# A hybrid decoder layer in fp32r: the moving operand of every wide matmul read by turns from two pieces

## The chip, the cores and the metric

The kernel runs on one core of one Trainium2 chip. The metric is the device time of one execution in microseconds (us). In the profile, PE is the matrix engine (TensorE), PEld its weight loads, DVE is VectorE, ACT is ScalarE, POOL is GpSimd and SP is SyncE, which issues most of the DMAs. L835 means line 835 of the kernel.

## The reference, cut to what matters

One layer (DEPTH is 1) on 1024 tokens of width 1024, all in float32:

```python
h = rms_norm(x, mix_norm)
z = h @ w_in                     # 1024 x 2320: gq gk gv gr glr sq sk sv
o_gla = rms_norm(gla_chunked(gq, gk, gv, log_a), gla_norm) * silu(gr)     # 4 heads
o_swa = swa_sink_attention(rms_norm(sq, q_norm), rms_norm(sk, k_norm), sv, sinks)   # window 128
x = x + concat([o_gla, o_swa]) @ w_out
u = causal_dwconv(rms_norm(x, ffn_norm) @ w_up, conv_w, conv_b)           # 1024 x 5632
a, bval = split(u, 2)
return x + (silu(a) * bval) @ w_down                                      # 2816 x 1024
```

## The kernel before, in words

The tokens are eight row tiles of 128. A matmul has a stationary operand of 128 x 128, which a weight load brings in ahead of it, and a moving operand of up to 512 columns, which is streamed past it; the result goes to a PSUM bank of 512 fp32 values. For accuracy each fp32 operand of a large matmul is split into a high part, rounded to the type fp32r, and the rest (`split`, line 92, and `tr_hi`/`tr_lo`, lines 250 and 258), and a product takes three passes: high by high, high by low, low by high.

The work runs in this order. *Input projections* (up to about 300 us): a tile of `x` is normalised and transposed into `big` (row tile, block of 128 features, high or low, 128 tokens); `dense` (line 314) multiplies eight feature blocks of `big`, stationary, with a weight block of 512 columns (272 for `k`), moving, 24 matmuls into one bank. `unit_q`, `unit_k`, `unit_v`, `unit_g` and `unit_r` take the bank and scale, square or multiply it (`head_rms`, `q_post`, `gla_qk`, `gate`). Between them stand the steps of the attention (`swa_scores`: queries stationary, 256 keys of `kt` moving, lines 443 and 444) and of the gated linear attention. *Output projection* (about 300 to 400 us): `unit_o` adds its bank to the residual `acc` and starts the second norm. Its rows are transposed into `big` again; for tiles 4 to 7, `norm2_sums` forms sums and differences of the quadrants in PSUM and puts them into `big` and `ex`.

*Feed-forward* (about 400 us to the end): both large products are done by a Strassen-Winograd scheme of seven products for a two by two block product. Up (`product`, line 822): the weights `w` are stationary, the moving operand (`b_operand`, line 801) is four row tiles of `big` or `ex`, 4 x 128 columns out of four places 8 KB apart in a partition; twelve matmuls into one bank. `post` combines the banks, and runs the convolution and the gate on DVE and ACT. Down (`down_pair`, line 1006): the gated tokens `g` are stationary, half a row block of `w_down` (512 columns) is moving; six matmuls into two banks, which one add of DVE over 1024 elements puts into `acc` (line 1020). `last_row` does the last two blocks of `w_down` row tile by row tile, and stores.

The order of the work is written out by hand: `at` gives each step a time, and the steps are issued in the order of these times; the first ones are a fixed list. On each engine the instructions run in the order of issue, with semaphores between engines. POOL and ACT split weights ahead of their use, DVE and ACT empty the banks.

Of the kernel before, what the change touches and what calls it, by code (L numbers as in the profile page):

```python
# [34 lines left out]
def hymba_layer_kernel(ctx, tc, x, mix_norm, w_in, w_alpha2, b_alpha, gla_norm,  # L35
# [175 lines left out]
    def norm2_tr(t):  # L211
        h = fin["h", t]
        if t < 4:
            norm_tr(t, h, "n2")
            return
        pbs = fin["pb", t] = []
        for q in range(2):
            pt = bank(f"n2pt_{t}_{q}")
            for k in range(4):
                c = (q * 4 + k) * P  # L220
                pe.transpose(pt[:, k * P:(k + 1) * P], h[:, c:c + P], ident)
            pbs.append(pt.rearrange("p (k c) -> p k c", k=4))

    def norm2_sums(t):

        i, ex, pn = t - 4, fin["ex"], fin["pn"]
        p0, p1 = fin["pb", t]

        def put(src, dst):
            split(src, dst[:, :, 0, :], dst[:, :, 1, :], dve)  # L230

        b12 = pn.tile([P, 4, P], F32, tag="b12", name=f"b12_{t}", bufs=1)
        b11, b21 = big[:, i, 0:4].bitcast(F32), big[:, i, 4:8].bitcast(F32)
        act.copy(b12, p0)
        put(p1, big[:, t, 4:8])
        dve.tensor_sub(p0, p0, b11[:, :, 0, :])
        dve.tensor_sub(p0, p0, b11[:, :, 1, :])
        put(p0, big[:, t, 0:4])
        dve.tensor_sub(p1, p1, b12)
        put(p1, ex[:, 1, i])  # L240
        dve.tensor_add(p1, p1, b11[:, :, 0, :])
        dve.tensor_add(p1, p1, b11[:, :, 1, :])
        put(p1, ex[:, 0, i])
        dve.tensor_sub(p0, b21[:, :, 0, :], p1)
        dve.tensor_add(p0, p0, b21[:, :, 1, :])
        put(p0, ex[:, 2, i])

    trs = {}

    def tr_hi(t, q, h, tag):  # L250
# [5 lines left out]
        act.copy(big[:, t, q * 4:q * 4 + 4, 0, :], trs[tag, t, q])  # L256

    def tr_lo(t, q, tag):
        hi, lo = big[:, t, q * 4:q * 4 + 4, 0, :], big[:, t, q * 4:q * 4 + 4, 1, :]
        dve.tensor_sub(lo, trs[tag, t, q], hi.bitcast(F32))  # L260

    def norm_tr(t, h, tag):
        for q in range(2):
            tr_hi(t, q, h, tag)
            tr_lo(t, q, tag)


    blocks = {}
# [41 lines left out]
    def load_piece(name, c0, n, k2, engs=(None, None), hi_eng=None):  # L310
# [3 lines left out]
    def dense(t, ws, n, name):  # L314
        pb = bank(name)
        for k in range(KD):
            for i, (ra, rb) in enumerate(PASSES):
                pe.matmul(pb[:, :n], lhsT=big[:, t, k, ra, :], rhs=ws[k][:, rb, :n],  # L318
                          start=(k == 0 and i == 0), stop=(k == KD - 1 and i == 2))
        return pb  # L320


    qo = gl_q.tile([P, NT, 512], F32, name="qo")
# [31 lines left out]

    def head_rms(ps_ap, nh, t, name):
        sq = k2_tile(name + "sq")
        act.activation(sq[:, :nh * HD], ps_ap, AF.Square, scale=row_scale(t))
        ss = gl.tile([P, 8], F32, tag="hss", name=name + "ss", bufs=3)
        dve.tensor_reduce(ss[:, :nh], sq[:, :nh * HD].rearrange("p (h d) -> p h d", d=HD),  # L360
                          op=ALU.add, axis=AX.X)
        return rms_scale(ss[:, :nh], HD, nh, name, gl, f"hr{nh}")

    def q_post(t, pb):
        r = head_rms(pb, 8, t, f"q{t}")
        rs = gl.tile([P, 8], F32, tag="rs", name=f"rs{t}", bufs=2)
        dve.scalar_tensor_tensor(rs, r, row_scale(t), qscale, op0=ALU.mult, op1=ALU.mult)
        dve.tensor_tensor(
            qo[:, t, :].rearrange("p (j g d) -> p g j d", j=4, g=2),
            pb.rearrange("p (g j d) -> p g j d", g=2, j=4),  # L370
            rs.rearrange("p (g j o) -> p g j o", g=2, o=1).broadcast_to((P, 2, 4, HD)),
            ALU.mult)

# [61 lines left out]
    def swa_scores(t, g):  # L435
# [3 lines left out]
        for j in range(4):  # L439
            if j % 2 == 0:  # L440
                pbs.append(bank(f"sc{t}_{g}_{j}").rearrange("p (j s) -> p j s", j=2))
            qc, kc = slice(j * P, (j + 1) * P), slice(t * P, t * P + 256)
            pe.matmul(pbs[-1][:, j % 2, :], lhsT=q[:, g, qc], rhs=kt[:, g, kc], start=True, stop=False)  # L443
            pe.matmul(pbs[-1][:, j % 2, :], lhsT=ql[:, g, qc], rhs=kt[:, g, kc], start=False, stop=True)
        if g == 0:
            smx[t] = [gl.tile([P, 8], F32, tag=f"sm{i}", name=f"sm{i}_{t}", bufs=2) for i in range(4)]
        mx, nm, den, es = smx[t]
        pr = k4_tile(f"pr{t}_{g}").rearrange("p (j s) -> p j s", j=4)
        for j in range(4):
            h = g * 4 + j  # L450
            dve.tensor_tensor_reduce(pr[:, j, s0:], pbs[j // 2][:, j % 2, s0:], dist[:, s0:], 1.0,
                                     sinks_s[:, h:h + 1], ALU.add, ALU.max, mx[:, h:h + 1])
        hs = slice(g * 4, g * 4 + 4)
        dve.tensor_mul(nm[:, hs], mx[:, hs], slope_n[:, hs])
# [95 lines left out]
    def gla_qk(t, pb):  # L550
        ex = gex[t]
        kd = gkd[t] = gl.tile([P, 256], F32, tag="kd", name=f"kd{t}", bufs=2)
        qe = gqk[t] = k2_tile(f"qe{t}")[:, 0:256]
        for i, dst, c, e in ((1, qe, 0, 0), (0, kd, 256, 1)):
            dve.scalar_tensor_tensor(dst, pb[:, c:c + 256], row_scale(t, i), ex[:, e], op0=ALU.mult, op1=ALU.mult)

    def gla_tr(t):
        pb = bank(f"gt{t}")
# [142 lines left out]
    def unit_q_part(t, k0, k1):  # L701
        if k0 == 0:
            psb["q", t] = bank(f"dq{t}")
        pb = psb["q", t]
        for k in range(k0, k1):

            for i, (ra, rb) in enumerate(((0, 0), (1, 0), (0, 1))):
                pe.matmul(pb, lhsT=big[:, t, k, ra, :], rhs=blocks["q"][k][:, rb, :],  # L708
                          start=(k == 0 and i == 0), stop=(k == KD - 1 and i == 2))

    def q_done(t):
        q_post(t, psb.pop(("q", t)))

    def unit_q(t):
        q_post(t, dense(t, blocks["q"], 512, f"dq{t}"))
# [2 lines left out]
        kvl_post(t, dense(t, blocks["k"], 272, f"dk{t}"))  # L718

    def unit_v(t):  # L720
        act.activation(vg[0][:, t, :], dense(t, blocks["v"], 512, f"dv{t}"), AF.Copy, scale=row_scale(t))

    def unit_g(t):
        gla_qk(t, dense(t, blocks["g"], 512, f"dg{t}"))
# [4 lines left out]
    def unit_o(t, half):  # L729
# [5 lines left out]
        dve.tensor_add(acc[:, cs], acc[:, cs], pb)  # L735
        if half == 1:
            norm2_stat(t)

# [83 lines left out]
    def product(ch, name):  # L822
# [9 lines left out]
        if ch == 0:  # L832
            steps.sort(key=lambda step: step[2])
        for i, (k, ra, rb) in enumerate(steps):
            pe.matmul(pb, lhsT=w[:, ra, k, :], rhs=b_operand(bn, k, rb),  # L835
                      start=(onto is None and i == 0), stop=(i == 11), skip_group_check=onto is not None)

    def half_tile(name):
# [167 lines left out]
    def down_pair(p, k, j):  # L1006
# [6 lines left out]
        for i in range(2):  # L1013
            for n, (ra, rb) in enumerate(PASSES):
                c = (2 * j + i) * P
                pe.matmul(pb[:, i], lhsT=g[:, ra, c:c + P], rhs=w[:, rb, :],  # L1016
                          start=(onto is None and n == 0), stop=(n == 2), skip_group_check=onto is not None)
        t = 4 * th + 2 * j
        acc = fin["all"][:, t:t + 2, nh * 512:(nh + 1) * 512]
        dve.tensor_add(acc, acc, pb)  # L1020

    def w_split(ch, hf, slot):
        w = blocks["d", ch, hf] = slot_tile(slot, f"dnw{ch}_{hf}")
# [9 lines left out]
    def last_row(t):  # L1033
# [6 lines left out]
        for hf, pb in enumerate(pbs):  # L1040
            for c0, c1 in ((0, 256), (256, 512)) if (t, hf) == (NT - 1, 1) else ((0, 512),):
                for ch in (NCH - 2, NCH - 1):
                    g, w = gtiles[ch, t // 4], blocks["d", ch, hf]
                    for i, (ra, rb) in enumerate(PASSES[::-1]):
                        pe.matmul(pb[:, c0:c1], lhsT=g[:, ra, (t % 4) * P:(t % 4 + 1) * P], rhs=w[:, rb, c0:c1],  # L1045
                                  start=(ch == NCH - 2 and i == 0), stop=(ch == NCH - 1 and i == 2))
                cs = slice(hf * 512 + c0, hf * 512 + c1)
                dve.tensor_add(acc[:, cs], acc[:, cs], pb[:, c0:c1])
                sp.dma_start(out[t * P:(t + 1) * P, cs], acc[:, cs])


# [253 lines left out]
```

## Time and profile before

| | |
|---|---|
| median of 3 runs | 1033.62 us (1032.31 to 1033.64) |
| the profiled execution | 1033.08 us, its span 1031.4 us |
| granted TensorE clock, mean | 0.999 of full |
| busy share of the span | PE 99%, PEld 82%, DVE 77%, POOL 60%, ACT 47% |
| matmuls | 4976, each with a weight load of its own |
| DMA | 67.13 MB, 65 GB/s on the mean |

Matmuls are pipelined: one starts long before the one ahead has ended. So the mean duration of a matmul in the profile (389 ns for 512 columns) is a latency, and its cost is the time from its start to the start of the next. A busy time of a group is the union of its members' times.

### The profile page before, as it was taken

The numbers are of one execution on the slowest core, as the hardware profiler recorded it, in microseconds if no ns is written. First come the engines' busy times: TensorE is split into PE (matmuls) and PEld (weight loads), VectorE is DVE, ScalarE is ACT, GpSimd is POOL, SyncE is SP. The second block draws the span as 40 slices with busy tenths as digits, with TensorE's granted clock in tenths as the row PEclk, the third lists the DMA queues.
The fourth block names the chain that finished last, engine by engine and source line by source line (L and its number), as shares of the span: only waits on it lengthen the run. The fifth ranks groups of instructions, "written<-read, shape, count | busy, mean of one in ns | idle before, by whom it ended". The sixth has DMA issues, their size and how long they took to land.

```text
span 1031.4 us, 13921 instructions
## 1 busy us (share of the span) xinstructions
PE 1023.9 (99%) x4976; PEld 849.5 (82%) x4976; DVE 795.6 (77%) x1332; ACT 480.7 (47%) x988; POOL 618.3 (60%) x510
## 2 busy tenths in 40 slices
PE   9999999999999999999999999999999999999998
PEld 6899887888888888888888888888888888888887
DVE  6776667764131689797989899897979898998976
ACT  5627655445240345554444545444444444454541
POOL 4592132325560205867878797887878787978750
PEclk9999999999999999999999999999999999999999
DMA  6252113002035202112120212212121111122104
GB/s 218 61 155 62 42 45 102 21 1 83 1 101 185 62 1 82 41 42 83 41 71 33 62 41 62 62 48 75 41 82 41 63 41 44 59 62 62 42 20 163
DMA packets 67502, 67.13 MB, mean 65 GB/s; under 512 B 4648, under 2 KB 52201, under 8 KB 67434
## 3 DMA queue, kind: packets, MB, share of 16 engines
q1 hardware_dynamic: 63448, 61.27, 19.3%
q10 hardware_dynamic: 3986, 4.99, 2.0%
q8 instruction: 39, 0.64, 0.2%
q14 instruction: 29, 0.24, 0.1%
HBM read 57.33 MB, written 4.19 MB: 60 GB/s over the span
## 4 chain that ended last, share of the span: by engine, by line
PE 96%; DVE 2%; ACT 1%; DMA 0%; issue 0%; POOL 0%; ACTq 0%; SPq 0%
PE fb L835 38%; PE dn_P L1016 18%; PE do L318 8%; PE dg L318 4%; PE dr L318 4%; PE dv L318 4%; PE dq L318 3%; PE dk L318 2%; PE gb L835 2%; PE dq L708 1%; PE pv L491 1%; PE dl L1045 1%; PE fb L1045 1%; PE go L601 1%; PE ga L592 1%; PE sc L443 1%
## 5 line engine op out<-in xcount | busy, mean ns | idle before, releaser
L1016 PE MATMUL dn_P<-dw,dg 128*128 128x512 f32 x840 | 212.9, 389 | 0.0
L1020 DVE TENSOR_TENSOR acc<-acc,dn_P 128x1024 f32<-128x1024 f32 x140 | 169.7, 1213 | 55.7 <-PE dn_P L1016 55.5
L1016 PEld LDWEIGHTS dn_P<-dw,dg 128*128 128x128 f32 x840 | 157.6, 188 | 33.1 <-DVE acc L1020 0.4
L318 PE MATMUL do<-wow,big 128*128 128x512 f32 x384 | 90.9, 393 | 0.0
L97 POOL TENSOR_TENSOR dw<-dn,dw 128x512 fp32r<-128x512 f32 x50 | 68.8, 1377 | 25.1 <-ACT dw L94 24.1
L318 PEld LDWEIGHTS do<-wow,big 128*128 128x128 f32 x384 | 71.1, 188 | 14.4
L887 ACT COPY ca<-fb 128x512 f32<-128x512 f32 x62 | 36.3, 586 | 65.0 <-PE fb L835 65.0
L842 DVE SCALAR_TENSOR_TENSOR ua<-fb,cc,ua 128x511 f32<-128x511 f32 x84 | 62.2, 741 | 0.3
L835 PE MATMUL fb<-big,A11w 128*128 128x512 f32 x252 | 61.2, 389 | 0.0
L835 PE MATMUL fb<-big,A12w 128*128 128x512 f32 x252 | 60.9, 390 | 0.2 <-DVE ua L842 0.2
L835 PE MATMUL fb<-big,S4w 128*128 128x512 f32 x252 | 61.0, 389 | 0.0
L835 PE MATMUL fb<-big,S1w 128*128 128x512 f32 x252 | 61.0, 389 | 0.0
L835 PE MATMUL fb<-ex,S3w 128*128 128x512 f32 x252 | 60.9, 389 | 0.0
L835 PE MATMUL fb<-ex,S2w 128*128 128x512 f32 x252 | 60.9, 389 | 0.0
L835 PE MATMUL fb<-ex,A22w 128*128 128x512 f32 x252 | 60.5, 389 | 0.0
L835 PEld LDWEIGHTS fb<-big,A12w 128*128 128x128 f32 x252 | 47.1, 188 | 10.3 <-DVE ua L842 0.6
L835 PEld LDWEIGHTS fb<-ex,S3w 128*128 128x128 f32 x252 | 47.3, 188 | 9.8
L835 PEld LDWEIGHTS fb<-big,S1w 128*128 128x128 f32 x252 | 47.3, 188 | 9.8
L835 PEld LDWEIGHTS fb<-ex,A22w 128*128 128x128 f32 x252 | 47.3, 188 | 9.8
L835 PEld LDWEIGHTS fb<-ex,S2w 128*128 128x128 f32 x252 | 47.3, 188 | 9.8
L835 PEld LDWEIGHTS fb<-big,A11w 128*128 128x128 f32 x252 | 47.3, 188 | 9.8
L835 PEld LDWEIGHTS fb<-big,S4w 128*128 128x128 f32 x252 | 47.3, 188 | 9.8
(432 smaller groups left out, 2395.6 us busy)
## 6 DMA issues: line engine op xcount, KB each, us to landing
up<-in_w_up_dram SPq DMA_DIRECT2D x44, 512.0 KB, 3.9
dn<-in_w_down_dram SPq DMA_DIRECT2D x22, 512.0 KB, 3.5
acc<-in_x_dram SPq DMA_DIRECT2D x8, 512.0 KB, 6.6
out_dram<-acc SPq DMA_DIRECT2D x15, 256.0 KB, 2.0
xt<-in_x_dram SPq DMA_DIRECT2D x7, 512.0 KB, 3.6
vraw<-in_w_in_dram SPq DMA_DIRECT2D x4, 512.0 KB, 3.9
graw<-in_w_in_dram SPq DMA_DIRECT2D x4, 512.0 KB, 3.7
qt<-qt ACTq DMA_DIRECT2D x16, 128.0 KB, 2.2
```

What stands on the lines that cost most here:

```text
L97: (eng or pool).tensor_sub(lo, src, hi.bitcast(F32))
L318: pe.matmul(pb[:, :n], lhsT=big[:, t, k, ra, :], rhs=ws[k][:, rb, :n], start=(k == 0 and i == 0), stop=(k == KD - 1 and i == 2))
L443: pe.matmul(pbs[-1][:, j % 2, :], lhsT=q[:, g, qc], rhs=kt[:, g, kc], start=True, stop=False)
L491: pe.matmul(pbs[i][HALF[g]], lhsT=vv[rows, t - 1 + b, HALF[g]], rhs=rhs[rows, :, HALF[i]], start=start, stop=stop)
L592: pe.matmul(pb[:, pr * 256:(pr + 1) * 256], lhsT=gqt[t][:, pr, :], rhs=qbd[t % 2][:, pr], start=(pr == 0), stop=(pr == 1))
L601: pe.matmul(pb[:, h * P:(h + 1) * P], lhsT=asb[:, h, :], rhs=v[:, h * P:(h + 1) * P], start=(h == 0), stop=(t == 0 and h == 3))
L835: pe.matmul(pb, lhsT=w[:, ra, k, :], rhs=b_operand(bn, k, rb), start=(onto is None and i == 0), stop=(i == 11), skip_group_check=onto is n ...
L842: dve.scalar_tensor_tensor(dst, src, w, dst, op0=ALU.mult, op1=ALU.add)
L887: act.copy(dst, pb)
L1016: pe.matmul(pb[:, i], lhsT=g[:, ra, c:c + P], rhs=w[:, rb, :], start=(onto is None and n == 0), stop=(n == 2), skip_group_check=onto is no ...
L1020: dve.tensor_add(acc, acc, pb)
L1045: pe.matmul(pb[:, c0:c1], lhsT=g[:, ra, (t % 4) * P:(t % 4 + 1) * P], rhs=w[:, rb, c0:c1], start=(ch == NCH - 2 and i == 0), stop=(ch == N ...
```

## The change

The order in which each wide moving operand is read is altered, and the data is laid out so that the results come out right.

- Weights (`dense`, `unit_q_part`, `down_pair`, `last_row`): the 512 columns stay where they are, and are read 0, 256, 1, 257, and so on. Column c of the first half is then at place 2c of the bank, column c of the second half at 2c + 1. All that takes such a bank reads it with a step of two, first half and second half in turn, and writes in the old order.
- The `k` weights (272 columns) are put apart when they are split: even columns into the first half, odd ones into the second. Read by turns they come out in the old order, and the bank is as it was.
- The keys `kt` (256 columns, two blocks of 128) are read by turns, and the scores taken with a step of two.
- The activations of the up products: in each row tile of `big` and `ex`, even tokens stand in the first 64 places and odd ones in the last 64, for the second norm only (`parted`). The transposed tile is taken out of PSUM with a step of two, and `norm2_sums` works through such views throughout. `product` reads the two sets of a row tile by turns, so that the tokens of a bank are in the old order.

Stationary operands are read as before, and the number of instructions, waits and DMAs is as it was. The diff, cut to its core:

```diff
+    def two_streams(a):
+        return a.rearrange("p (h c) -> p c h", h=2)
+
+    def halves_of(pb):
+        return pb.rearrange("p (c h) -> p h c", h=2)
...
 norm2_sums
-            split(src, dst[:, :, 0, :], dst[:, :, 1, :], dve)
+            dst = dst.rearrange("p k r (h c) -> p k r h c", h=2)
+            split(src, dst[:, :, 0], dst[:, :, 1], dve)
...
 tr_hi
+        if parted:
+            trs[tag, t, q] = pt.rearrange("p (k c h) -> p k h c", k=4, h=2)
+        act.copy(tr_dst(t, q, 0, parted), trs[tag, t, q])
...
 piece
+            if name == "k":
+                src = halves_of(src)
+                hi, lo = (part.rearrange("p (h c) -> p h c", h=2) for part in (hi, lo))
...
 dense
-                pe.matmul(pb[:, :n], lhsT=big[:, t, k, ra, :], rhs=ws[k][:, rb, :n],
+                pe.matmul(pb[:, :n], lhsT=big[:, t, k, ra, :], rhs=two_streams(ws[k][:, rb, :n]),
...
-        return pb
+        return halves_of(pb) if n == 512 else pb
...
 swa_scores
-            pe.matmul(pbs[-1][:, j % 2, :], lhsT=q[:, g, qc], rhs=kt[:, g, kc], start=True, stop=False)
+            pe.matmul(pbs[-1][:, j % 2, :], lhsT=q[:, g, qc], rhs=two_streams(kt[:, g, kc]), start=True, stop=False)
...
 product
-            pe.matmul(pb, lhsT=w[:, ra, k, :], rhs=b_operand(bn, k, rb),
+            pe.matmul(pb, lhsT=w[:, ra, k, :], rhs=b_operand(bn, k, rb).rearrange("p t (h c) -> p t c h", h=2),
...
 down_pair
-                pe.matmul(pb[:, i], lhsT=g[:, ra, c:c + P], rhs=w[:, rb, :],
+                pe.matmul(pb[:, i], lhsT=g[:, ra, c:c + P], rhs=two_streams(w[:, rb, :]),
...
-        acc = fin["all"][:, t:t + 2, nh * 512:(nh + 1) * 512]
-        dve.tensor_add(acc, acc, pb)
+        acc = fin["all"][:, t:t + 2, nh * 512:(nh + 1) * 512].rearrange("p i (h c) -> p i h c", h=2)
+        dve.tensor_add(acc, acc, pb.rearrange("p i (c h) -> p i h c", h=2))
```

`unit_q_part` and `last_row` change as `dense` and `down_pair` do; `head_rms`, `q_post`, `gla_qk`, `gate`, `unit_v` and `unit_o` take their banks through the halves.

More of the change, by code (lines that the diff above doesn't have):

```diff
@@ L213, in norm2_tr @@
         if t < 4:
-            norm_tr(t, h, "n2")
+            norm_tr(t, h, "n2", True)
             return
@@ L221, in norm2_tr @@
                 pe.transpose(pt[:, k * P:(k + 1) * P], h[:, c:c + P], ident)
[L222 removed]
+            pbs.append(pt.rearrange("p (k c h) -> p k h c", k=4, h=2))
     def norm2_sums(t):
@@ L229, in put @@
         def put(src, dst):
-            split(src, dst[:, :, 0, :], dst[:, :, 1, :], dve)
-        b12 = pn.tile([P, 4, P], F32, tag="b12", name=f"b12_{t}", bufs=1)
-        b11, b21 = big[:, i, 0:4].bitcast(F32), big[:, i, 4:8].bitcast(F32)
+            dst = dst.rearrange("p k r (h c) -> p k r h c", h=2)
+            split(src, dst[:, :, 0], dst[:, :, 1], dve)
+        b12 = pn.tile([P, 4, 2, P // 2], F32, tag="b12", name=f"b12_{t}", bufs=1)
+        b11, b21 = (big[:, i, c:c + 4].bitcast(F32).rearrange("p k r (h c) -> p k r h c", h=2) for c in (0, 4))
         act.copy(b12, p0)
         put(p1, big[:, t, 4:8])
-        dve.tensor_sub(p0, p0, b11[:, :, 0, :])
-        dve.tensor_sub(p0, p0, b11[:, :, 1, :])
+        dve.tensor_sub(p0, p0, b11[:, :, 0])
+        dve.tensor_sub(p0, p0, b11[:, :, 1])
         put(p0, big[:, t, 0:4])
@@ L240, in norm2_sums, with tr_hi @@
         put(p1, ex[:, 1, i])
-        dve.tensor_add(p1, p1, b11[:, :, 0, :])
-        dve.tensor_add(p1, p1, b11[:, :, 1, :])
+        dve.tensor_add(p1, p1, b11[:, :, 0])
+        dve.tensor_add(p1, p1, b11[:, :, 1])
         put(p1, ex[:, 0, i])
-        dve.tensor_sub(p0, b21[:, :, 0, :], p1)
-        dve.tensor_add(p0, p0, b21[:, :, 1, :])
+        dve.tensor_sub(p0, b21[:, :, 0], p1)
+        dve.tensor_add(p0, p0, b21[:, :, 1])
         put(p0, ex[:, 2, i])
     trs = {}
-    def tr_hi(t, q, h, tag):
+    def tr_hi(t, q, h, tag, parted=False):
         pt = bank(f"{tag}pt_{t}_{q}")
@@ L255, in tr_hi, with tr_dst, tr_lo, norm_tr @@
         trs[tag, t, q] = pt.rearrange("p (k c) -> p k c", k=4)
-        act.copy(big[:, t, q * 4:q * 4 + 4, 0, :], trs[tag, t, q])
-    def tr_lo(t, q, tag):
-        hi, lo = big[:, t, q * 4:q * 4 + 4, 0, :], big[:, t, q * 4:q * 4 + 4, 1, :]
+        if parted:
+            trs[tag, t, q] = pt.rearrange("p (k c h) -> p k h c", k=4, h=2)
+        act.copy(tr_dst(t, q, 0, parted), trs[tag, t, q])
+    def tr_dst(t, q, r, parted):
+        dst = big[:, t, q * 4:q * 4 + 4, r, :]
+        return dst.rearrange("p k (h c) -> p k h c", h=2) if parted else dst
+    def tr_lo(t, q, tag, parted=False):
+        hi, lo = (tr_dst(t, q, r, parted) for r in range(2))
         dve.tensor_sub(lo, trs[tag, t, q], hi.bitcast(F32))
-    def norm_tr(t, h, tag):
+    def norm_tr(t, h, tag, parted=False):
         for q in range(2):
-            tr_hi(t, q, h, tag)
-            tr_lo(t, q, tag)
+            tr_hi(t, q, h, tag, parted)
+            tr_lo(t, q, tag, parted)
     blocks = {}
@@ L442, in swa_scores @@
             qc, kc = slice(j * P, (j + 1) * P), slice(t * P, t * P + 256)
-            pe.matmul(pbs[-1][:, j % 2, :], lhsT=q[:, g, qc], rhs=kt[:, g, kc], start=True, stop=False)
-            pe.matmul(pbs[-1][:, j % 2, :], lhsT=ql[:, g, qc], rhs=kt[:, g, kc], start=False, stop=True)
+            pe.matmul(pbs[-1][:, j % 2, :], lhsT=q[:, g, qc], rhs=two_streams(kt[:, g, kc]), start=True, stop=False)
+            pe.matmul(pbs[-1][:, j % 2, :], lhsT=ql[:, g, qc], rhs=two_streams(kt[:, g, kc]), start=False, stop=True)
         if g == 0:
@@ L553, in gla_qk @@
         qe = gqk[t] = k2_tile(f"qe{t}")[:, 0:256]
-        for i, dst, c, e in ((1, qe, 0, 0), (0, kd, 256, 1)):
-            dve.scalar_tensor_tensor(dst, pb[:, c:c + 256], row_scale(t, i), ex[:, e], op0=ALU.mult, op1=ALU.mult)
+        for i, dst, e in ((1, qe, 0), (0, kd, 1)):
+            dve.scalar_tensor_tensor(dst, pb[:, e], row_scale(t, i), ex[:, e], op0=ALU.mult, op1=ALU.mult)
     def gla_tr(t):
@@ L707, in unit_q_part @@
             for i, (ra, rb) in enumerate(((0, 0), (1, 0), (0, 1))):
-                pe.matmul(pb, lhsT=big[:, t, k, ra, :], rhs=blocks["q"][k][:, rb, :],
+                pe.matmul(pb, lhsT=big[:, t, k, ra, :], rhs=two_streams(blocks["q"][k][:, rb, :]),
                           start=(k == 0 and i == 0), stop=(k == KD - 1 and i == 2))
     def q_done(t):
-        q_post(t, psb.pop(("q", t)))
+        q_post(t, halves_of(psb.pop(("q", t))))
     def unit_q(t):
@@ L720, in unit_v @@
     def unit_v(t):
-        act.activation(vg[0][:, t, :], dense(t, blocks["v"], 512, f"dv{t}"), AF.Copy, scale=row_scale(t))
+        act.activation(vg[0][:, t, :].rearrange("p (h c) -> p h c", h=2), dense(t, blocks["v"], 512, f"dv{t}"),
+                       AF.Copy, scale=row_scale(t))
     def unit_g(t):
@@ L734, in unit_o @@
         pb = dense(t, blocks[f"o{half}"], 512, f"do{half}_{t}")
-        dve.tensor_add(acc[:, cs], acc[:, cs], pb)
+        part = acc[:, cs].rearrange("p (h c) -> p h c", h=2)
+        dve.tensor_add(part, part, pb)
         if half == 1:
@@ L1044, in last_row @@
                     for i, (ra, rb) in enumerate(PASSES[::-1]):
-                        pe.matmul(pb[:, c0:c1], lhsT=g[:, ra, (t % 4) * P:(t % 4 + 1) * P], rhs=w[:, rb, c0:c1],
+                        pe.matmul(pb[:, c0:c1], lhsT=g[:, ra, (t % 4) * P:(t % 4 + 1) * P], rhs=two_streams(w[:, rb, c0:c1]),
                                   start=(ch == NCH - 2 and i == 0), stop=(ch == NCH - 1 and i == 2))
                 cs = slice(hf * 512 + c0, hf * 512 + c1)
-                dve.tensor_add(acc[:, cs], acc[:, cs], pb[:, c0:c1])
+                part = acc[:, cs].rearrange("p (h c) -> p h c", h=2)
+                dve.tensor_add(part, part, halves_of(pb[:, c0:c1]))
                 sp.dma_start(out[t * P:(t + 1) * P, cs], acc[:, cs])
```

14 lines of the change are left out of this document (9 added, 5 removed).

## Prediction

> **What bounds the kernel now.** I read the page first (shares, then the chain of waits), then TensorE's own waits, then stages, then the distance between matmul starts.
>
> ```profile
> span 1031.4 us, 13921 instructions
> PE 1023.9 (99%) x4976; PEld 849.5 (82%) x4976; DVE 795.6 (77%) x1332; ACT 480.7 (47%) x988; POOL 618.3 (60%) x510
> PE 96%; DVE 2%; ACT 1%; DMA 0%; issue 0%; POOL 0%; ACTq 0%; SPq 0%
> ```
>
> The profiled execution took 1033.08 us, 1.7 us around its span of 1031.4; the median of the three runs shown is 1033.62, 0.5 us more. A difference under 0.2% (2 us) can't be told from none with this kernel. The chain is TensorE (PE) for 96%. All waits that the trace shows for PE, from the longest to the shortest, are six:
>
> ```profile
> PE warm L1086 <- DVE warm L125: 1.7, 1, 1.7
> PE dg L318 <- ACT vg L721: 1.2, 1, 1.2
> ...
> PE fb L835 <- DVE ua L842: 0.2, 1, 0.2
> ```
>
> They sum to 3.8 us. So no other engine matters unless it becomes late; the time is the number of matmuls times the distance from one start to the next. That distance (the pitch) is read from unbroken runs: the chain gives a run from start to start; in the timeline a run of n lasts n-1 pitches and one duration, whose mean the groups give.
>
> ```profile
> 482.13 2.72 PE fb L835 x12
> 60.24 13.92 PE L318 MATMUL dk<-kw,big 128*128 128x272 f32 x110
> L318 PE MATMUL dk<-kw,big 128*128 128x272 f32 x192 | 25.2, 290 | 0.0
> 1026.99 0.87 PE L1045 MATMUL fb<-dnw,g 128*128 128x256 f32 x6
> L1045 PE MATMUL fb<-dnw,g 128*128 128x256 f32 x12 | 1.7, 282 | 0.0
> 79.34 0.60 PE L411 MATMUL za<-wa,gt 128*128 128x256 f32 x2
> L411 PE MATMUL za<-wa,gt 128*128 128x256 f32 x16 | 4.8, 379 | 0.0
> ```
>
> 512 columns (fp32r operands): 2.72/12 = 226.7 ns. 272 columns: (13.92 - 0.290)/109 = 125.1. 256 columns: (0.87 - 0.282)/5 = 117.6. From 272 to 512 a column costs (226.7 - 125.1)/240 = 0.423 ns, and what is left is 226.7 - 512 x 0.423 = 9.9 ns on every matmul, whatever its width. The last group are matmuls of plain fp32 operands (the others are fp32r): 0.60 - 0.379 = 221 ns for 256 columns, 0.863 ns a column. They take a 4-byte element at half the pace of the fp32r matmuls.
>
> So a wide matmul here streams a column in 0.423 ns and loses some 10 ns more. Those 10 ns are all that a change of the read order can win; what it can lose has no such lid.
>
> **The change, part by part.**
>
> *The matmuls.* No instruction is added, removed or moved, no wait and no DMA. What changes is the order of addresses in the moving operand: element c of one piece, element c of the other, c+1 of the first, and so on, the pieces 256, 136, 128 or 64 elements apart. How many matmuls:
>
> ```profile
> 0.00:1031.40 1031.40, 442.64 (x1848) 346.54 (x1848) 1.00 0.22 65
> 0.00:1031.40 1031.40, 284.48 (x1272) 224.41 (x1272) 1.00 0.22 65
> 0.00:1031.40 1031.40, 212.92 (x840) 157.58 (x840) 1.00 0.22 65
> 0.00:1031.40 1031.40, 22.19 (x102) 18.46 (x102) 1.00 0.22 65
> L708 PE MATMUL dq<-qw,big 128*128 128x512 f32 x72 | 19.3, 405 | 0.6 <-POOL qw L296 0.3 <-DVE big L260 0.2
> L443 PE MATMUL sc<-kt,qt 128*128 128x256 f32 x64 | 17.4, 304 | 0.0
> L444 PE MATMUL sc<-kt,ql 128*128 128x256 f32 x64 | 15.7, 282 | 0.0
> ```
>
> The first four rows are the whole span for lines 835 (up products), 318 (dense units), 1016 (down products) and 1045 (last rows). With 192 of line 318 at 272 columns and 12 of line 1045 at 256: 1848 + 1080 + 840 + 90 + 72 = 3930 matmuls of 512, 192 of 272, 128 + 12 of 256; 4262 in all.
>
> No matmul of this trace alternates, so the price is bounded from both sides. Below: all 9.9 ns go, 4262 x 9.9 = 42 us. Above: each element costs what a plain fp32 column does, 0.863 - 0.423 = 0.440 ns more: (3930 x 512 + 192 x 272 + 140 x 256) x 0.440 = 924 us. I take the lower end, and this is the choice on which the forecast rests. The up products' operand is already four runs of 128 elements from four row tiles, and it has the 226.7 ns of unbroken operands, so a jump in the address is not in itself dear. And the loss looks like one of reading, not of starting a matmul: 256 plain fp32 columns at two passes of 0.423 ns would be 216.6 of their 221 ns, so some 4 ns are left there (the 0.60 is rounded, so from none to 9), with the same weight load beside each. At half the read pace the array seems to pay less of the extra. What is lost is then read time at full pace while weights load alongside, and two pieces may let one be fetched while the other is held up. That is an inference, not a row.
>
> [...]
>
> *Weight loads* stay as they are.
>
> ```profile
> 301.06 0.60 PE L624 MATMUL ogt<-ident,gs 128*128 128x128 f32 x4
> L624 PE MATMUL ogt<-ident,gs 128*128 128x128 f32 x32 | 4.8, 271 | 0.0
> L1016 PEld LDWEIGHTS dn_P<-dw,dg 128*128 128x128 f32 x840 | 157.6, 188 | 33.1 <-DVE acc L1020 0.4
> ```
>
> A load lasts 188 ns by its record, yet four transposes, each with a load of its own, follow at (0.60 - 0.271)/3 = 110 ns. So loads would hold no matmul at 217 ns, nor the 272-column ones at 115.
>
> *Evictions.* Where weights are in halves, the result lies interleaved in PSUM, and VectorE (DVE) and ScalarE (ACT) read first every even, then every odd element; DVE also reads and writes the transposed tiles that way in the norm2 sums.
>
> ```profile
> 434.00:1000.00 566.00, 565.82 (x2496) 467.89 (x2495) 503.97 (x628) 271.28 (x462) 442.26 (x324) 1.00 0.18 54
> 434.00:1000.00 566.00, 169.02 (x140) 1.00 0.18 54
> L1020 DVE TENSOR_TENSOR acc<-acc,dn_P 128x1024 f32<-128x1024 f32 x140 | 169.7, 1213 | 55.7 <-PE dn_P L1016 55.5
> L735 DVE TENSOR_TENSOR acc<-acc,do 128x512 f32<-128x512 f32 x16 | 10.9, 684 | 26.7 <-PE do L318 20.7 <-DMA acc<-in_x_dram 6.0
> L368 DVE TENSOR_TENSOR qo<-dq,rs 128x512 f32<-128x512 f32 x8 | 5.5, 688 | 0.2
> L721 ACT ACTIVATE vg<-dv,rn 128x512 f32<-128x512 f32 x8 | 5.5, 687 | 5.7 <-PE dv L318 5.6
> ```
>
> An add of 1024 elements takes 1213 ns, one of 512 takes 684: 1.03 ns an element. Lower bound 0; the other bound is half speed, 1024 x 1.03 = 1.06 us more on each of the 140 adds of line 1020. I take 0: the multiplication of line 368 writes in runs of 64 and costs 688, as much as contiguous ones (a step on the read side no row has). The cover is DVE's free time: 566 - 504 = 62 us in this stage, 37 when the stage shrinks by 25, which is 0.26 us an add. ACT's evictions, eight each of 0.69 us for v and the gate, have an engine at 47%.
>
> *Operands stored apart.* The eight k splits read their source with a step of two, and the copies after the norm2 transposes write in another order:
>
> ```profile
> L94 ACT CAST kw<-kraw 128x272 fp32r<-128x272 f32 x8 | 2.8, 432 | 1.6 <-DMA kraw<-in_w_in_dram 1.6
> 394.57 0.68 DVE L239 TENSOR_TENSOR n2pt<-n2pt,b 128x512 f32<-128x512 f32 x1
> 397.00:466.00 69.00, 68.79 (x306) 56.37 (x306) 60.44 (x94) 37.63 (x66) 50.12 (x39) 1.00 0.19 54
> ```
>
> I cost them at nothing; at double price the splits are 3.5 us on ACT, hidden, and a last tile's eleven norm2 steps of 0.68 would be up to 6 us later where DVE is at 60.4 of 69.
>
> *The sum.* 42 us, less 0.7 for the 72 matmuls of line 708, whose pace weights from other engines set, less about 3 for new waits: from 434 to 1000 us PE would need 2496 x 9.9 ns = 25 us less, DVE would go from 89% to 504/541 = 93%, and the adds, which free the banks that the next down product needs, come late more easily. That leaves 38: 1033 - 38 = **995 us**, its own range 978 to 1015 (11 ns and no new wait, to half of the loss regained).
>
> **The rivals.**
>
> *Each element is a new fetch (slower).* Place: every wide matmul; price: up to 0.440 ns an element, 924 us as above, **1957 us**; it decides from a pitch above 226.7, so from 4% over the streaming pace. For it: nothing in the trace alternates, the shortest run is 64 elements, and the fp32r stream runs at twice the pace of any other 4-byte one here, so it has the least slack. Against it: breaks every 128 elements are free. [...]
>
> *The 9.9 ns belong to the start of a matmul (no change).* Then the read order is indifferent: **1033 us**. For it: the loss is the same per matmul at 272 and 512 columns. Against it: the 4 ns of plain fp32, though rounding leaves room for 9.
>
> *DVE becomes the bound (slower).* If reading every second element of PSUM halves its speed, the stage needs 504 + 140 x 1.06 = 652 us of DVE in place of 566; with 17 us still won elsewhere, 1033 + 86 - 17 = **1102 us**. It decides from 0.26 us an add on. For it: DVE is the second busiest engine there; against it: line 368.
>
> **How the numbers follow.** Forecast 0.61, at any size of gain over 2 us; no change 0.14; new fetches 0.15; DVE 0.05; a small loss up to 1060 us, from evictions that are partly slower, 0.05. So faster 0.61, same 0.14, slower 0.25. The range 978 to 1060 leaves out the two large losses, 0.20 together; it holds cases of both signs, and so the forecast's own range stands above.
>
> **What would show it.** Right: runs of twelve up products in about 2.60 us instead of 2.72, the 272-column run at 115 ns; the line 1020 group at 1.21 us; PE still above 95% of the chain. Wrong: twelve in 2.72 (no change) or in 3 to 5.3 us (new fetches); line 1020 near 2.2 us with PE waiting for it (DVE). The forecast falls if the reader of the moving operand keeps only one line at a time, or if DVE's waits eat more than 3 us.

## The result, and the profile after

The changed kernel takes 994.43 us (993.8 to 996.48 in four runs), the one before 1033.13 on the same chip: a ratio of 0.963, 95% interval 0.9613 to 0.9646. The forecast was 995. The profiled execution's span is 992.1 us, 39.3 less. From its page, the span, the busy shares and the chain's shares:

```profile
span 992.1 us, 13927 instructions
PE 980.5 (99%) x4976; PEld 850.6 (86%) x4976; DVE 789.2 (80%) x1332; ACT 481.4 (49%) x988; POOL 613.4 (62%) x510
PE 85%; DVE 9%; POOL 2%; ACT 1%; issue 1%; DMA 1%; ACTq 0%; POOLq 0%; DVEq 0%; SPq 0%
```

The list of waits, for the weight loads of PE (waiting line, releasing line: us in all, number, longest):

```profile
PEld dn_P L1038 <- DVE acc L1042: 3.0, 8, 1.1
```

The same work is on PE, and the matmuls follow each other faster. An unbroken run of the chain of waits (start, us, number):

```profile
462.52 2.59 PE fb L857 x12
```

The 272-column run on the timeline (start, us from the first start to the last end), and then its group (us, mean ns):

```profile
58.59 12.90 PE L335 MATMUL dk<-kw,big 128*128 128x272 f32 x110
```

```profile
L335 PE MATMUL dk<-kw,big 128*128 128x272 f32 x192 | 23.4, 281 | 0.0
```

512 columns: 2.59/12 = 215.8 ns, where it was 226.7. 272 columns: (12.90 - 0.281)/109 = 115.8, where it was 125.1. The engines that empty the banks, and the `k` splits (groups by line, mean ns of one):

```profile
L1042 DVE TENSOR_TENSOR acc<-acc,dn_P 128x1024 f32<-128x1024 f32 x140 | 169.3, 1211 | 32.5 <-PE dn_P L1038 32.4
L741 ACT ACTIVATE vg<-dv,rn 128x512 f32<-128x512 f32 x8 | 5.5, 688 | 4.4 <-PE dv L335 4.3
L100 ACT CAST kw<-kraw 128x272 fp32r<-128x272 f32 x8 | 3.8, 566 | 2.1 <-DMA kraw<-in_w_in_dram 2.1
```

A step of two in PSUM cost nothing here: 1211 ns after 1213, 688 after 687. A step of two in SBUF, which only the splits of the `k` weights have, took the eight copies on ACT from 432 to 566 ns; 1.1 us in all, on an engine at 49%. The subtractions of these splits, on POOL, read with the same step and stayed at 779 ns, where they took 772.

New is that DVE shows up on the chain with 9%, while PE's share falls from 96% to 85%, and that the down products' weight loads wait for the adds of line 1042 eight times, 3.0 us, where it was once, 0.4. DVE's idle time ahead of these adds went from 55.7 to 32.5 us.

### The profile page after: what moved, and what is told of

It is laid out like the page before. It is cut to its first block, busy times and chain, and to the rows that moved or that the text cites. A ratio compares the mean times of both kernels' runs of the same rounds, so it can differ in the third digit from the quotient of the medians.

```text
span 992.1 us, 13927 instructions
## 1 busy us (share of the span) xinstructions
PE 980.5 (99%) x4976; PEld 850.6 (86%) x4976; DVE 789.2 (80%) x1332; ACT 481.4 (49%) x988; POOL 613.4 (62%) x510
## 4 chain that ended last, share of the span: by engine, by line
PE 85%; DVE 9%; POOL 2%; ACT 1%; issue 1%; DMA 1%; ACTq 0%; POOLq 0%; DVEq 0%; SPq 0%
PE fb L857 36%; PE dn_P L1038 18%; PE do L335 6%; PE dg L335 4%; PE dr L335 4%; PE dv L335 3%; PE dq L335 2%; PE dq L728 1%; PE pv L511 1%; PE dl L1067 1%; PE fb L1067 1%; DVE n2h L214 1%; PE gb L857 1%; DVE acc L1042 1%; PE go L621 1%
## 5 line engine op out<-in xcount | busy, mean ns | idle before, releaser
L1038 PE MATMUL dn_P<-dw,dg 128*128 128x512 f32 x840 | 205.0, 380 | 1.0 <-DVE acc L1042 0.7
L1042 DVE TENSOR_TENSOR acc<-acc,dn_P 128x1024 f32<-128x1024 f32 x140 | 169.3, 1211 | 32.5 <-PE dn_P L1038 32.4
L103 POOL TENSOR_TENSOR dw<-dn,dw 128x512 fp32r<-128x512 f32 x50 | 65.1, 1301 | 35.9 <-ACT dw L100 35.9
L335 PE MATMUL do<-wow,big 128*128 128x512 f32 x384 | 86.2, 382 | 0.0
L857 PE MATMUL fb<-big,A11w 128*128 128x512 f32 x252 | 58.5, 379 | 0.0
L857 PE MATMUL fb<-big,S1w 128*128 128x512 f32 x252 | 58.3, 379 | 0.0
L857 PE MATMUL fb<-big,S4w 128*128 128x512 f32 x252 | 58.3, 379 | 0.0
L857 PE MATMUL fb<-ex,S2w 128*128 128x512 f32 x252 | 58.1, 379 | 0.0
L857 PE MATMUL fb<-ex,S3w 128*128 128x512 f32 x252 | 58.1, 379 | 0.0
L857 PE MATMUL fb<-ex,A22w 128*128 128x512 f32 x252 | 57.8, 379 | 0.0
L869 ACT ACTIVATE ua<-fb,cc 128x512 f32<-128x512 f32 x42 | 32.7, 779 | 45.6 <-DVE fb L917 29.9
```

The lines of the kernel that those rows point to most:

```text
L103: (eng or pool).tensor_sub(lo, src, hi.bitcast(F32))
L335: pe.matmul(pb[:, :n], lhsT=big[:, t, k, ra, :], rhs=two_streams(ws[k][:, rb, :n]), start=(k == 0 and i == 0), stop=(k == KD - 1 and i == 2))
L857: pe.matmul(pb, lhsT=w[:, ra, k, :], rhs=b_operand(bn, k, rb).rearrange("p t (h c) -> p t c h", h=2), start=(onto is None and i == 0), sto ...
L869: act.activation(u[:, a:z], y[:, a:z], AF.Identity, bias=b, scale=w2)
L1038: pe.matmul(pb[:, i], lhsT=g[:, ra, c:c + P], rhs=two_streams(w[:, rb, :]), start=(onto is None and n == 0), stop=(n == 2), skip_group_che ...
L1042: dve.tensor_add(acc, acc, pb.rearrange("p i (c h) -> p i h c", h=2))
```

## The experiments

**1. The whole kernel: the order of the reads, or the layout?** Two complementary kernels. One has the new layout and evictions with unbroken reads:

```diff
     def two_streams(a):
-        return a.rearrange("p (h c) -> p c h", h=2)
+        return a
...
 product
-                      rhs=b_operand(bn, k, rb).rearrange("p t (h c) -> p t c h", h=2),
+                      rhs=b_operand(bn, k, rb),
```

> Everything as in the changed kernel (evictions with a step of two, operands stored apart), but every moving operand is read unbroken; values come out in permuted places. If the whole gain is the order of the reads and the strided evictions are free: 1033 us, ratio to before 0.998 to 1.002, pitch 226.7, DVE add of 1024 elements 1.21 us. Rival: the new evictions cost something that the gain hides: over 1035. Other rival: part of the gain comes from the layout (fewer conflicts when banks are emptied): under 1031.

The other is the kernel before with `two_streams` put around every wide moving operand, and nothing else touched.

> The kernel before with nothing altered but the order of the moving reads; evictions and stored order are the old ones, so values come out in permuted places. If evictions are free: 994 us, the changed kernel's time, within 0.3%. Rival (strided evictions cost DVE time that makes PE wait): 988 to 992.

Measured: 1033.25 us, ratio 1.0004 (0.9994 to 1.0013), and 994.8 us, ratio 0.963 (0.9616 to 0.9645). Of the new layout read unbroken, a run of twelve up products from the chain, and the add of 1024 elements from the groups:

```profile
481.87 2.72 PE fb L857 x12
```

```profile
L1042 DVE TENSOR_TENSOR acc<-acc,dn_P 128x1024 f32<-128x1024 f32 x140 | 169.7, 1213 | 55.7 <-PE dn_P L1038 55.4
```

The same two of the kernel before read by turns:

```profile
481.58 2.59 PE fb L838 x12
```

```profile
L1023 DVE TENSOR_TENSOR acc<-acc,dn_P 128x1024 f32<-128x1024 f32 x140 | 169.4, 1211 | 33.5 <-PE dn_P L1019 33.4
```

So, within the 1 us or so that the intervals leave open, the whole gain is the order of the reads, and all that serves it is free.

**2. One part undone: the up products alone read unbroken** (the second half of the diff above).

> The changed kernel with the up products' operand alone read unbroken (tokens of a bank permuted). Per-matmul theory: 1848 x 10.9 ns = 20.1 us come back, so 1014 to 1015 us, with the up matmuls at 226.7 and all others at 215.8. Rival (the up products' four runs of 128 in places 8 KB apart gain less, or gain is not additive since waits in that stage vanish with the slower pace): 1008 to 1012.

Measured: 1013.03 us, ratio 0.9804 (0.9787 to 0.982). From its chain, a down unit and the up product behind it:

```profile
481.50 1.29 PE dn_P L1038 x6
482.79 2.73 PE fb L857 x12
```

Down products stay at 1.29/6 = 215 ns, up products go back to 227 or so. Against the changed kernel, 18.6 us come back by the times and 18.0 by the ratios, instead of 20.1. That fits a price per matmul, less some waits that vanish at the slower pace. The intervals, about 2 us to either side, don't settle the difference; experiment 6 counts these waits in the traces.

**3. The matmuls alone: what is it that gets faster?** Two suspects of the prediction were a fixed cost of each matmul, and reads held up by the weight load alongside. A kernel that only runs matmuls, 25 in a row of each form (13 of plain fp32, of which each leaves two records), all on data of `w_up` with eight stationary tiles in turn. It was run once, as were those of experiments 4 and 5. The forms, written here as functions:

```python
def halves(n): return mv[:, 0:n].rearrange("p (h c) -> p c h", h=2)             # L45, L117
def dist(d):   return mv[:, 0:512].rearrange("p (a h c) -> p a c h", h=2, c=d)   # 2: L49, 4: L53
def step(s):   return mv[:, 0:512 * s].rearrange("p (c s) -> p s c", s=s)[:, 0]  # 2: L77
```

> A kernel of matmul runs alone, 25 each of one form, with nothing else on the chip; the layer is left out. Theory A (the 11 ns are moving reads held up by the weight load that runs alongside): unbroken 226.7 ns, halves by turns 215.8; with a stationary operand of 64 columns the unbroken loss halves (221), with 32 it is a quarter (218.5); with the stationary columns 32 bytes apart, so that each is fetched singly, unbroken gets worse (240 or more); widths of 256 and 384 lose the same 11 to 13 ns, and by turns none; plain fp32 and bf16 show no difference. Theory B (a fixed cost of starting an unbroken read): 226.7 with 64 and 32 stationary columns and with the spread load too. Theory C (a stall of the stream itself at every so many bytes, whatever the load does): the loss goes with the width, 5.5 ns at 256 and 8 at 384. [...] On distance A says that from 4 elements on it works, at 2 it doesn't.

The timeline of PE. From the start of one form to the start of the next are 25 pitches; where a run is taken by itself, the mean duration of one is taken off, and one pitch fewer counted:

```profile
23.75 5.83 PE L41 MATMUL plain<-mv,st 128*128 128x512 f32 x25
29.42 5.56 PE L45 MATMUL halves<-mv,st 128*128 128x512 f32 x25
34.82 5.85 PE L49 MATMUL dist<-mv,st 128*128 128x512 f32 x25
40.50 5.56 PE L53 MATMUL dist<-mv,st 128*128 128x512 f32 x25
45.90 5.56 PE L57 MATMUL dist<-mv,st 128*128 128x512 f32 x25
...
62.08 7.25 PE L69 MATMUL quarters<-mv,st 128*128 128x512 f32 x25
...
81.32 11.48 PE L77 MATMUL step<-mv,st 128*128 128x512 f32 x25
92.63 11.71 PE L81 MATMUL step<-mv,st 128*128 128x512 f32 x25
...
140.91 5.92 PE L113 MATMUL plainM<-mv,st 128*64 128x512 f32 x25
146.67 5.56 PE L117 MATMUL halvesM<-mv,st 128*64 128x512 f32 x25
...
175.10 5.57 PE L137 MATMUL bf<-mb,sb 128*128 128x512 bf16 x25
180.51 12.27 PE L141 MATMUL bfhalves<-mb,sb 128*128 128x512 bf16 x25
192.62 11.32 PE L145 MATMUL full<-mf,sf 128*128 128x512 f32 x26
203.78 14.20 PE L149 MATMUL fullhalves<-mf,sf 128*128 128x512 f32 x26
```

| moving operand, 512 columns | from | ns |
|---|---|---|
| fp32r unbroken | (29.42 - 23.75)/25 | 226.8 |
| fp32r, halves by turns | (34.82 - 29.42)/25 | 216.0 |
| by turns at a distance of 2 elements | (40.50 - 34.82)/25 | 227.2 |
| by turns at a distance of 4 elements | (45.90 - 40.50)/25 | 216.0 |
| by turns from four pieces | (7.25 - 0.451)/24 | 283.3 |
| one piece with a step of 2 | (92.63 - 81.32)/25 | 452.4 |
| unbroken, 64 stationary columns | (146.67 - 140.91)/25 | 230.4 |
| bf16 unbroken | (180.51 - 175.10)/25 | 216.4 |
| bf16, halves by turns | (192.62 - 180.51)/25 | 484.4 |
| plain fp32 unbroken, each record | (11.32 - 0.592)/25 | 429.1 |
| plain fp32, halves by turns, each record | (14.20 - 0.703)/25 | 539.9 |

The empty chip shows the kernel's two pitches (226.8 and 216.0 ns), so nothing of the other engines is in them. Theory A falls as it was stated: with half the weights to load the loss isn't halved, it grows from 10.8 to some 14 ns. Its guess on the distance (2 doesn't help, 4 does) came true, but experiments 4 and 5 point elsewhere, and its guess that bf16 and plain fp32 are indifferent was badly off (216.4 to 484.4 and 429.1 to 539.9). Neither A nor C has the widths right: beside a full weight load the loss is some 8 ns at 256 columns, 12 at 384 and 11 at 512, which is neither constant nor in step with the columns. A distance of 2 elements, 8 bytes, is too near (227.2 ns), and one of 4, 16 bytes, is far enough (216.0). From here on a *line* is a unit of counting: 16 adjacent bytes of the operand, four fp32r elements or eight of bf16. That the hardware reads by such lines was not shown; the runs show pitches. A line serves the columns that pass while it is in use. A step of two, which takes two elements of each line, doubles the time (452.4).

**4. Does the loss belong to the matmul or to its columns?** Again matmuls alone, with 32 stationary columns (49 in a row), a quarter of the weights to load; steps of two by turns from two halves; fp32r and bf16 in blocks of 2, 4, 8 and 32 elements by turns; one or two lines read over and over; weights spread 8 bytes apart.

> Runs of matmuls alone again, the layer left out. The first runs ruled out that the loss scales with the weights loaded alongside (230 ns with 64 columns, 231 with 32) or with the width. Theory B (starting an unbroken read costs some 11 to 16 ns, once per matmul): pieces by turns in blocks of 8 or 32 elements give 226 to 231, as the start is unbroken; one 16-byte line read over and over gives 226 or more; with 32 stationary columns every width from 128 to 512 loses the same amount against halves by turns. Theory D (the reader keeps two lines, and an unbroken read has to wait at lines it steps into): one line read over and over gives 215.8, blocks of 2 elements 215.8, blocks of 4 (a line of one, a line of the other) 226.7, and the loss shrinks with short widths. The two-line reader also says that the pieces need not change lines together: pieces at a distance of 257 and 258 elements, or both starting one element late, stay within 5 ns of 215.8. Steps of two by turns from two halves: 430 or more, since steps of two alone gave 452. bf16 by turns in blocks of 2 elements (4 bytes): if what counts is 4-byte units, near 216; if what counts is line changes, 300 or more, falling to 216 in blocks of 32. Weights spread 8 bytes apart: a change of the unbroken pitch and none of the other would bring the weight load back in.

```profile
35.99 8.50 PE L49 MATMUL grain<-mv,st 128*128 128x512 f32 x25
44.31 6.44 PE L53 MATMUL grain<-mv,st 128*128 128x512 f32 x25
...
62.59 5.63 PE L65 MATMUL oneline<-mv,st 128*128 128x512 f32 x25
68.06 5.61 PE L69 MATMUL twolines<-mv,st 128*128 128x512 f32 x25
...
94.07 5.85 PE L89 MATMUL stephalves<-mv,st 128*128 128x512 f32 x25
99.76 1.73 PE L93 MATMUL shortplain<-mv,st 128*32 128x64 f32 x49
...
102.87 3.11 PE L101 MATMUL shortplain<-mv,st 128*32 128x128 f32 x49
105.82 2.90 PE L105 MATMUL shorthalves<-mv,st 128*32 128x128 f32 x49
108.56 4.49 PE L109 MATMUL shortplain<-mv,st 128*32 128x192 f32 x49
...
149.94 11.50 PE L133 MATMUL shortplain<-mv,st 128*32 128x512 f32 x49
161.28 10.74 PE L137 MATMUL shorthalves<-mv,st 128*32 128x512 f32 x49
171.86 6.95 PE L141 MATMUL bfgrain<-mb,sb 128*128 128x512 bf16 x25
178.64 5.83 PE L145 MATMUL bfgrain<-mb,sb 128*128 128x512 bf16 x25
184.31 5.56 PE L149 MATMUL bfgrain<-mb,sb 128*128 128x512 bf16 x25
189.71 5.56 PE L153 MATMUL bfgrain<-mb,sb 128*128 128x512 bf16 x25
...
201.16 5.99 PE L161 MATMUL spread2plain<-mv,st 128*128 128x512 f32 x25
206.98 5.56 PE L165 MATMUL spread2halves<-mv,st 128*128 128x512 f32 x25
```

At 128 columns unbroken takes (105.82 - 102.87)/49 = 60.2 ns and halves (108.56 - 105.82)/49 = 55.9; at 512 it is 231.4 and 215.9. The loss is 4.3 and 15.5 ns: beside this small load it goes with the columns between these two widths, by 0.03 ns each. Theory B falls too. The constant that I read off two widths holds only beside a full weight load, where the loss is 9.3 ns at 272 columns and 10.9 at 512. Of theory C, that the stream itself stalls at every so many bytes, this much is left: the pitch goes with the columns that a line serves. That it is a stall was not shown. Steps of two by turns from two halves take (99.76 - 94.07)/25 = 227.6, half of the 452 of a single piece, and as much as an unbroken operand (226.8): in both a line serves four columns. And bf16, which has eight elements in 16 bytes, gives 271 in blocks of 2, (184.31 - 178.64)/25 = 226.8 in blocks of 4, 216.0 in blocks of 8: where four columns in a row come from a line it has the very pitch of unbroken fp32r, and where eight do, that of unbroken bf16 (216.4).

Two lines of fp32r read over and over, four columns of the one and four of the other, take (5.61 - 0.379)/24 = 218 ns. One line alone takes (68.06 - 62.59)/25 = 218.8. So a change of line every four columns cost nothing where the same two lines came back; an unbroken read, where each line is a new one, takes 226.8. That is in keeping with the two lines that theory D has the reader keep, which no run shows directly. Against D are its blocks: of 2 elements by turns it expected 215.8 and got (44.31 - 35.99)/25 = 332.8; blocks of 4, 8 and 32 took 251, 243 and 237, all dearer than an unbroken read (226.8), though a line serves four columns or more in each.

Nor is the weight load out of it. With weights spread 8 bytes apart the unbroken pitch is (206.98 - 201.16)/25 = 232.8, and halves by turns, (5.56 - 0.379)/24 = 215.9, stay as they were. By the recorded expectation this brings the load back in: not as the whole cause, but as something that at 8 bytes makes an unbroken read dearer and leaves the read by turns alone. At 32 bytes both are dearer: 246.8 unbroken (experiment 3's kernel, line 129) and 249.6 by turns (line 157 here). How is open.

**5. How many columns must a line serve?** The dial turned by itself: of every second line only the first 1, 2, 3 or 4 elements are used, by turns from two pieces (lines 49 to 61), or the first 2, 4, 6 or 8 of every eight of one piece (lines 65 to 77); and an unbroken operand with each pair read twice (line 81).

> Runs of matmuls alone, the layer left out. Theory E, formed after the first two: fp32r elements are taken in pairs, the first and the second of a pair by readers of their own, and what counts is how many pairs in a row each reader finds in one 16-byte line: four are free, two cost 11 ns in 512, one doubles the time. Two pieces by turns that skip every second line, with 1, 2, 3, 4 elements used of each line: 430 to 460, 227, between 216 and 227 (for 510 columns), 215.8. One piece with 2, 4 and 8 elements used in a row, again skipping lines: 2 (one pair a line) 430 to 460; 4 and 8 (two pairs a line) 227. Each pair of an unbroken operand read twice: four pairs a line, 216. Distance 2 and 4: 227 and 216. Rival F, one reader that holds two lines and gains whenever successive elements alternate between two lines: 1 and 2 elements of each line by turns both stay near 216 to 230, and the pair read twice stays at 227, since nothing alternates.

```profile
36.36 11.71 PE L49 MATMUL perline<-mv,st 128*128 128x512 f32 x25
47.89 5.96 PE L53 MATMUL perline<-mv,st 128*128 128x512 f32 x25
53.68 5.54 PE L57 MATMUL perline<-mv,st 128*128 128x510 f32 x25
59.06 5.56 PE L61 MATMUL perline<-mv,st 128*128 128x512 f32 x25
64.45 11.71 PE L65 MATMUL single<-mv,st 128*128 128x512 f32 x25
75.98 5.96 PE L69 MATMUL single<-mv,st 128*128 128x512 f32 x25
81.78 7.67 PE L73 MATMUL single<-mv,st 128*128 128x510 f32 x25
89.27 5.84 PE L77 MATMUL single<-mv,st 128*128 128x512 f32 x25
94.95 5.56 PE L81 MATMUL repeated<-mv,st 128*128 128x512 f32 x25
100.34 5.85 PE L85 MATMUL dist<-mv,st 128*128 128x512 f32 x25
```

| elements used of a line | two pieces by turns | one piece |
|---|---|---|
| 1 | (47.89 - 36.36)/25 = 461 | |
| 2 | (53.68 - 47.89)/25 = 232 | (75.98 - 64.45)/25 = 461 |
| 3 (510 columns) | (59.06 - 53.68)/25 = 215 | |
| 4 | (64.45 - 59.06)/25 = 216 | (81.78 - 75.98)/25 = 232 |

Two pieces by turns need half as many elements of a line for the same pitch. Counted in columns that pass while a line is in use, both columns of the table are one: two columns 461, four 232, six and eight free. Six of every eight elements of one piece, where a line lasts four columns and the next one two, lie between: (89.27 - 81.78)/25 = 300 for 510 columns. The pair read twice makes an unbroken line last eight columns, and it is free: (100.34 - 94.95)/25 = 216, with no second piece at all. Rival F falls on both counts.

So this is what the change does. An unbroken fp32r operand comes to a new line every four columns, and takes 226.8 ns. By turns from two pieces, two lines are in use at a time, each lasts eight columns, and it takes 216.0, some 5% less; bf16 by turns takes 484. Theory E, a reader for each of the two elements of a pair, fits the forms of the table and experiment 3's two pieces. No run shows such readers, and some forms speak against them: fp32r in four pieces by turns took 283 ns and in blocks of two elements 333, where by the theory each reader would come to another line at every access, as in the row of 461; blocks of 4 to 32 took 251 to 237, where it would have 227; and plain fp32 got worse by turns, from 429 to 540. The count of columns per line thus orders the fp32r pitches of one piece, and of two pieces taken element by element, and no more. How the reader works stays open.

**6. Where the rest of the gain went.** The pitches alone are worth 3930 x 10.9 + 192 x 9.3 = 44.6 us, and about one more at 256 columns; 39.3 arrived. To see whether DVE holds the rest, the two small convolution steps at the boundary between the token halves (`conv_edge`) are left out, from the changed kernel and from the one before, so that the first two tokens of the second half lack those taps.

> The changed kernel without the two small convolution steps at the token boundary in the middle (84 DVE instructions of 1 or 2 columns; the first two tokens of the second half lack those taps). The profile has PE idle for 11.6 us in the changed kernel and 7.5 in the one before. If the added 4 us are waits for a DVE that is at 91% from 434 to 1000 us: PE idle falls by 2 us or more there and the time to 990 to 992. Rival (they come from other places, or the order of the steps): 994, within 0.2%.

> The same steps left out of the kernel before: PE hardly waits for DVE there, so no change, 1032.5 to 1033.5 us.

The page counts 88 DVE instructions fewer (1332 to 1244), where the expectation has 84. Measured: 990.69 us, ratio 0.9593 (0.9577 to 0.9609), 3.7 us better than the changed kernel; and 1032.61, ratio 0.9997 (0.9988 to 1.0007), no change. The wait of the weight loads for the adds falls to 0.7 us (the group's row, its idle time last):

```profile
L1037 PEld LDWEIGHTS dn_P<-dw,dg 128*128 128x128 f32 x840 | 158.7, 189 | 23.2 <-DVE acc L1041 0.7
```

PE's idle time by the page fell by 1.2 us only, less than I expected. The page counts as busy a matmul's whole modelled duration, 379 ns at a pitch of 216, so a start that is late by less than 163 ns shows no idle time.

The starts themselves show it. From the first up product on, 2778 matmuls of 512 columns run. Adding up by how much the next start comes later than the usual pitch, wherever that is over 20 ns, gives 1.2 us in the kernel before (8 starts), 5.2 in the changed one (33; 6.2 in its second profile) and 2.4 without the two steps (12); late down products alone go from 2.5 us (20) to 0.6 (2). So about 4 of the 6 us are late starts in the feed-forward, and the two steps on DVE make most of these. The other 2 us or so arise ahead of it, and no run here tests what by. Experiment 2's kernel has 2.9 us (13), some 2 us less than the changed one; that is about what its price fell short by.

The same load can be taken off DVE without leaving anything out, on ACT, which is busy for 49%:

```diff
 conv_edge
-        tap(u[:, 0:1], e[:, 1:2], cc[:, 1, ci:ci + 1])
-        tap(u[:, 0:2], e[:, 0:2], cc[:, 0, ci:ci + 1])
+        for c, s, j in ((0, 1, 1), (0, 0, 0), (1, 1, 0)):
+            act.activation(u[:, c:c + 1], e[:, s:s + 1], AF.Identity, bias=u[:, c:c + 1], scale=cc[:, j, ci:ci + 1])
```

> The changed kernel, nothing left out: the two small convolution steps at the token boundary go from DVE to ACT (three ACTIVATE of one column in place of two DVE steps, 132 in all, on an engine that is busy for 49%). If DVE's load makes the new waits: some 27 us less of DVE work and 990.5 to 992 us. Rival: the hop from DVE to ACT and back ahead of the gate of the second half puts new waits into DVE's queue, and the time stays at 994 or above.

> Only the first half's edge steps go to ACT (66 ACTIVATE), where the SiLU that follows is on ACT already, so no hop is added. If DVE's load is the cause: about two thirds of the gain, 991 to 993 us; if hops matter, better than with both.

> The changed kernel itself once more, on the same chip as the two others, as their measure: 994.4 us, ratio to before 0.963.

Measured on one chip: 990.86 us with both moved (ratio to before 0.9591, 0.9578 to 0.9604), 992.92 with the steps of `a` alone (0.9613, 0.9599 to 0.9626; `a` is the half of the features that goes through `silu`), 994.97 for the changed kernel (0.963, 0.9617 to 0.9643). With both moved, the page's busy shares:

```profile
PE 977.1 (99%) x4976; PEld 851.2 (86%) x4976; DVE 768.2 (78%) x1244; ACT 522.3 (53%) x1120; POOL 619.5 (63%) x510
```

21 us less on DVE (27 were expected), 41 us more on ACT, and the best time of the kernels that compute the whole layer, 4.1 us under the changed one. Counted as above, late starts are 1.8 us (10), and no down product starts late. The hop to ACT and back did no visible harm. That moving the steps of `a` alone gives half of it is no more than a hint, as its interval overlaps with both others.

## Why the prediction was right, and where it was wrong

*What bounds the kernel* was right: PE's pitch set the time, and a change of the pitch by 4.8% moved the time by 3.7%.

*The lid on the gain*, some 10 ns a matmul, was about right in size; 42 us forecast, 45 to 46 worth by the new pitches. The term was a little too small because the split of 226.7 ns into columns and a fixed part was wrong: I took 0.423 ns a column and 9.9 ns fixed from two widths. By turns a column takes (215.8 - 115.8)/240 = 0.417 ns and 2.5 ns are fixed, so part of the loss lay in what I counted as streaming. Experiment 4 shows it in the columns beside 32 stationary ones; beside a full load it is neither in the columns nor fixed. The 11 ns at the lower end of the forecast's own range are shown by no row of the trace of before; the runs showed 10.9 at 512 columns and 9.3 at 272. (4262 x 11 ns is 47 us, which puts that end at 986, not 978.)

*The choice of the lower end* came out right on an argument of which one half was true. True was that the loss is one of reading: the order of the reads alone took the pitch from 226.7 ns to 215.8 (experiment 1). That it is one of the full pace was an inference, and no run tests it. Not borne out was the cause: fewer weights made the loss larger, not smaller (some 14 ns after 10.8, experiment 3), though the load has some part in it (232.8 ns with the weights 8 bytes apart, experiment 4). Nothing in the trace of before could tell that two pieces would be the right number, and it was a lucky choice in that sense: by the pitches of experiment 3, a step of two (452 ns) or four pieces (283) would have made the kernel slower.

*Evictions at nothing* was right, though line 368, which I leant on, had no step on its read side; experiment 1 shows it. *The k splits* cost 1.1 us where I had put nothing to 3.5, and they were hidden. The norm2 steps, feared to be up to 6 us, kept their times (684 ns after 681).

*What goes off the gain* was put at 3.7 us (0.7 for the matmuls of line 708, 3 for new waits) and was about 6. The adds of line 1042 came late, at the place that the prediction named, and experiment 6 brings back 3.7 to 4.1 us of it. So the time of 994.43 against 995 is closer than the terms: the gain was put 3 to 4 us too low and the losses some 2.5 too low, and the two errors nearly cancel. That part is luck.

*The signs.* The three on the pitches and the adds came out as forecast (2.59 us for twelve, 115.8 ns, 1.21 us). "PE still above 95% of the chain" did not: it is 85%, with DVE at 9%. And DVE's waits ate some 4 us by experiment 6, more than the 3 us at which, by the prediction's last line, the forecast falls. Its other condition, a reader that keeps only one line at a time, was a supposition; no run shows what the reader keeps, only that two pieces by turns take 215.8 ns. The time came so near to 995 because the larger gain paid for them.

*The rivals.* No change, as the loss belongs to the start of a matmul: excluded by the result, and by the widths of experiment 4. New fetches: reads at such a price exist (a step of two takes 452 ns, and the prediction's 226.7 + 512 x 0.440 comes to the same), but two pieces by turns escape it. DVE as the bound: the adds kept their 1.21 us; DVE is a cause of 4 us, not of 100.

## What to carry to other kernels

Where a kernel is bound by wide fp32r matmuls at 226.7 ns for 512 columns, read the moving operand element by element from two pieces at least 16 bytes apart: 215.8 ns (216.0 at 16 bytes, 227.2 at 8), and the evictions may take the resulting order with a step of two at no cost (1211 ns for an add of 1024 elements, after 1213). Don't carry it over to bf16 (484 ns) or plain fp32 (540 for 429), nor to steps of two (227.6 by turns), blocks (237 to 333) or four pieces (283). In fp32r reads of one piece, or of two taken element by element, count for how many columns each 16 bytes stay in use: 452 to 461 ns at two, 227 to 232 at four, 215 at six (measured with two pieces, 510 columns) and 216 at eight. Any other order is to be measured first. When the bounding engine gets faster, look at once for the next late one: here a DVE with 21 us less to do was worth another 4 us.

## What the runs showed of the hardware that was not expected

- fp32r, 512 columns: 452 to 461 ns when 16 bytes serve two columns, 227 to 232 at four, 216 at eight; bf16 in blocks of 4 and 8 elements by turns has the same 227 and 216, but in blocks of 2 it takes 271.
- fp32r with a step of two takes 452 ns although half of every 16 bytes is used; bf16 by turns from two halves takes 484.
- The loss of an unbroken operand is 10.9 ns beside a full weight load, but 15.5 beside one of 32 columns: fewer weights make it larger, and so do weights 8 bytes apart (232.8 ns, while the read by turns stays at 215.9). Why is open.
- Two times 16 bytes of fp32r read over and over, four columns each, take 218 ns: less than the 226.8 of an unbroken read, which comes to another 16 bytes as often.
- An SBUF read with a step of two slowed an ACT copy of 272 elements from 432 to 566 ns, while PSUM reads with a step of two cost DVE and ACT nothing (1211 ns after 1213, 688 after 687).
